# Memory keys and cross-attention queries of an encoder: high and low part of the moving operand side by side in 512 columns, the two halves added on the way out of PSUM

## The chip, the cores and the metric

The kernel runs on one core of a Trainium2 chip. The time is device microseconds of one execution; the number compared is the median of several runs. TensorE (PE) does the matmuls, VectorE (DVE) and ScalarE (ACT) the elementwise work, GpSimd (POOL) little here, and SyncE (SP) issues the loads. Sums of matmuls stand in PSUM, in banks of 128x512 numbers.

## The reference

Two layers of an encoder on 256 tokens of width 1024, with 256 tokens of memory. Cut to the part that matters here:

```python
for l in range(DEPTH):                       # DEPTH = 2
    h = hybrid_mixer(x, w_in[l], ...)
    x = layer_norm(alpha * x + h, ln_g[l, 0], ln_b[l, 0])
    h = memory_cross_attention(x, mem, xa_q[l], xa_kv[l], xa_o[l])
    x = layer_norm(alpha * x + h, ln_g[l, 1], ln_b[l, 1])
    h = conv_ffn(x, ffn_w_in[l], ...)
    x = layer_norm(alpha * x + h, ln_g[l, 2], ln_b[l, 2])

def memory_cross_attention(x, mem, xa_q, xa_kv, xa_o):
    q = (x @ xa_q).reshape(b, s, 4, 256) * 256 ** -0.5
    k, v = jnp.split(mem @ xa_kv, 2, axis=-1)
    p = softmax(q @ k^T)                     # per head
    return (p @ v).reshape(b, s, 1024) @ xa_o
```

The change touches `x @ xa_q` and the key half of `mem @ xa_kv`, 1024x1024 weights each, in both layers.

## The kernel before, in words

**Products.** Every f32 operand is split into a high part (a cast, L276, on ScalarE) and a low part (what is left, a subtraction, L277, on VectorE), and a product is three matmuls: high x high, high x low, low x high (`mm3`, L271 to L273). All weights pass once, in units of 128x1024 numbers (512 KB): SyncE's queue loads a unit into `raw`, ScalarE casts `hi`, VectorE subtracts `lo`. Seven units are prefetched, and eight `hi`/`lo` buffers exist.

**Two ways to use a unit.** Where the result is wanted with features on the partitions, `proj_f8` takes the unit's eight 128x128 blocks as stationary operands and the 256 tokens as the moving one: 24 matmuls of 256 columns into half a bank, so two units share one. The feed-forward uses `proj_twin` instead (L299, L301, L303). There the token activation is a `Twin`, which keeps high and low part of one block side by side, and one matmul of 512 columns multiplies the weight's high part with both: 8 matmuls of 512 columns, and 8 of 256 for the weight's low part times the high activation. A unit then fills a whole bank, with two halves that have to be added: `fold` copies one half out (L307, ScalarE) and adds the other to it (L308, VectorE). The accumulators `acc` are three banks; five more, `att`, hold transposes, attention and parts of the output projections.

**Stages.** Each layer: mixer, residual and LayerNorm, cross-attention, residual and LayerNorm, feed-forward, residual and LayerNorm. The LayerNorm (`ln`) of the two token tiles x_133 and x_134 takes sums (L409), a subtraction (L414), a reciprocal (L426) and a scaling (L419) on VectorE, with a square root on ScalarE (L410); TensorE then transposes the tile in pieces (L455), and each piece is split into high and low (L276, L277). Until then TensorE has no tokens for the next stage. The keys depend only on the memory, so their units fill such places: they stand in `fills`, and `main` allows some of them to be used at each LayerNorm. `split_keys` splits the finished keys (two tiles of 128x1024), ahead of the queries. The queries (`feat` under the name "xq") run right behind the LayerNorm, and after every two query units a head of the cross-attention is spawned (`cross_head`): scores, softmax (L871 to L879), transposes of the probabilities (L887), values.

**What sets the order.** `interleave` sets the steps one after another by rough costs. The framework then orders the instructions of each engine by a simulated schedule of its own; only SyncE's order is as written. LayerNorm operations are marked with `urgent`, and weight splits are kept `behind` them.

Of the kernel before, what the change touches and what calls it, by code (L numbers as in the profile page):

```python
# [111 lines left out]


def interleave(main, fills, banks):

    steps, done, active, pending = [], {}, [], []
    clock, free, nfill, allowed = 0.0, banks, 0, 0
    cur = next(main, None)

    def emit(s):  # L120
# [10 lines left out]
    while cur is not None or active:  # L131
# [23 lines left out]
        if isinstance(cur, Spawn):  # L155
            active.append([cur.name, clock + cur.delay, cur.gen, next(cur.gen)])
            cur = next(main, None)
            continue
# [66 lines left out]
class Encoder:  # L225
# [89 lines left out]
            self.mm3(o, xa.hi(kt + k, a, b), xa.lo(kt + k, a, b), hi[:, k], lo[:, k],  # L315
                     first and k == 0, last and k == 1)

    def feat(self, n, l, units, xn, evac):

        st = {}  # L320
        for i in range(units):
            def fn(u, i=i):
                if i % 2 == 0:
                    st["o"] = self.acc()
                o = st["o"]
                self.proj_f8(u, self.T[xn], o[:, 256 * (i % 2):256 * (i % 2) + 256])
                if i % 2:
                    evac(i // 2, o.rearrange("p (k t) -> p k t", k=2))
            yield Step(fn, U, units=[(n, l, i)])
# [135 lines left out]
    def fills(self):  # L465
        n = 0
        for l in range(DEPTH):
            def keys(l=l):
                for i in range(8):
                    def kfn(u, i=i):  # L470
                        if i == 0:
                            self.T["kT", l] = [self.big4() for _ in range(2)]
                        if i % 2 == 0:
                            self.T["ko"] = self.acc()
                        o = self.T["ko"]
                        self.proj_f8(u, self.T["mem"], o[:, 256 * (i % 2):256 * (i % 2) + 256])
                        if i % 2:
                            self.nc.scalar.copy(self.T["kT", l][i // 4][:, (i - 1) % 4:(i - 1) % 4 + 2],
                                                o.rearrange("p (k t) -> p k t", k=2))
                    yield ("k", l, i), Step(kfn, U, units=[("k", l, i)])  # L480

            def values(h, l=l):
                def evac(i, o):
                    if i == 0 and h == 0:
                        self.T["vM", l] = [[self.big(F32R) for _ in range(2)] for _ in range(2)]
                    vh, vl = self.T["vM", l]
                    sl = slice(512 * h, 512 * h + 512)
                    self.split_from(o, vh[i][:, sl], vl[i][:, sl])
                for s in self.tok("v", l, h, "mem", evac):
                    yield ("v", l, h), s  # L490

            parts = (values(0), keys(), values(1)) if l == 0 else (keys(), values(0), values(1))
            for p in parts:
                for k, s in p:
                    yield s
                    n += 1
                    self.nfill[k] = n
# [445 lines left out]
    def main(self):  # L943
        T = self.T
        allow = self.nfill
        yield Step(self.start)
        yield Allow(allow["k", 0, 3])
        for i in range(NT):
            yield Spawn(f"e{i}", self.ln(i, "xt00", 0, 15 + 5 * i))
        xn, lw = "xt00", ["e0", "e1"]  # L950
        for l in range(DEPTH):
            def lnc(j, l=l):
                return Step(lambda: self.ln_consts(self.aps["ln_g"][l, j], self.aps["ln_b"][l, j]))


            yield from self.tok_copy("va", l, xn, tiles=lw)
            if l == 0:
                yield Step(self.constants)
            rd = 6
            yield from self.feat_copy("qa", l, xn)  # L960
            yield Spawn(f"q{l}", self.rope("qa"), rd)
            yield from self.feat_copy("ka", l, xn)
            yield Spawn(f"k{l}", self.rope("ka"), rd)
            shs = [{"n": 0}, {"n": 0}, {"m": 0}]
            for i in range(NT):
                for g in range(2):
                    yield Spawn(f"dg{l}{i}{g}", self.diff_group(l, i, g, shs), 12)
            yield from self.tok_copy("vb", l, xn, split=True)
            yield from self.conv_branch(l, xn)
            yield from self.feat("qb", l, 4, xn, self.stack_evac("qb"))  # L970
            yield from self.feat("kb", l, 4, xn, self.stack_evac("kb"))
            yield Step(lambda l=l: self.bias_tiles(l, 0))
            for t in range(4):
                yield Spawn(f"na{l}{t}", self.near_pair(l, t), 1.0)
            yield from self.branch(l, 2, ("yc", l), xn, first=True)
            yield Wait(f"da{l}")
            yield from self.branch(l, 0, ("ya", l), xn)
            yield Wait(*(f"na{l}{t}" for t in range(4)))
            yield from self.branch(l, 1, ("yb", l), xn, last=True)
            yield lnc(0)  # L980
            yield Allow(max(allow["v", l, 0], allow["k", l, 7]))
            yield Step(self.load_mem)
            xn = f"xt{l}1"
            yield from self.residual(self.tok_out("mo", l, ("mg", l)), f"m{l}", xn)

            yield Wait(f"m{l}0", f"m{l}1")
            yield Allow(allow["v", l, 1])

            def evac(q, o):
                if q == 0:  # L990
                    T["qx"] = Act([self.big4(F32R)], [self.big4(F32R)])
                elif q == 2:
                    T["qx"].his.append(self.big4(F32R))
                    T["qx"].los.append(self.big4(F32R))
                f = 2 * (q % 2)
                self.split_from(o, T["qx"].his[-1][:, f:f + 2], T["qx"].los[-1][:, f:f + 2])
            yield Step(lambda l=l: self.split_keys(l))
            for n, s in enumerate(self.feat("xq", l, 8, xn, evac)):
                yield s
                if n % 2:  # L1000
                    yield Spawn(f"x{l}{n // 2}", self.cross_head(l, n // 2), 1.0)
            yield Wait(*(f"x{l}{h}" for h in range(4)))
            yield lnc(1)
            yield Allow(allow["k", 1, 3])
            xn = f"xt{l}2"
            yield from self.residual(self.tok_out("xo", l, ("oT", l)), f"a{l}", xn)

            um = l == DEPTH - 1
            if um:
                yield Step(self.keep_warm, acq=1, rel=1)  # L1010
                yield from self.up_first(l, xn, [f"a{l}0", f"a{l}1"])
            yield Wait(f"a{l}0", f"a{l}1")
            yield from self.ffn_in(l, xn, 4 if um else 0)
            yield Allow(allow["k", 1, 7])
            last = l == DEPTH - 1
            xn = None if last else f"xt{l + 1}0"
            lw = [f"f{l}0", f"f{l}1"]
            yield from self.residual(self.ffn_out(l), f"f{l}", xn)
        yield Wait(*lw)
# [239 lines left out]
```

## Time and profile before

| | |
|---|---|
| median of 3 runs | 1127.05 us (1126.41 to 1127.45) |
| profiled execution | 1126.91 us |
| its span in the trace | 1125.1 us |
| mean granted clock of TensorE | 0.994 |
| busy: TensorE / VectorE / ScalarE / GpSimd | 1094.9 / 833.2 / 643.4 / 12.4 us |
| loads | 208.45 MB, 185 GB/s over the span |

In the rows that follow, a row of a timeline has the start, the duration, engine, line, operation, output<-input, the size, how many such instructions stand together, and in brackets the idle time of the engine ahead of it and what ended it. A row of the groups has the busy time, the mean in ns, and the idle time in front with its releaser. Consecutive matmuls overlap, so their price is the distance between their starts, not the duration.

### The profile page before, as it was taken

The page shows a single profiled execution, that of the slowest core. Times are in us where ns is not written, and L with a number is a line of the kernel's source. Part 1 is how long each engine was busy: PE and PEld are TensorE (multiplying, and loading weights), DVE is VectorE, ACT ScalarE, POOL GpSimd, SP SyncE. Part 2 cuts the span into 40 slices and gives each one's busy share as a digit, 9 for nine tenths or more (in the row PEclk, how much of TensorE's full clock was granted, in tenths as well). Part 3 has the DMA queues.
Part 4 walks back from the last instruction along what each step waited for, and adds up shares of the span by engine and source line. Part 5 has one row for each costly group of instructions (what it writes and reads, how often), then busy time and mean ns, then how long its engine had stood idle before and what let it go on. Part 6 is the DMA issues. An engine that isn't in the chain of part 4 may idle for free.

```text
span 1125.1 us, 17377 instructions
## 1 busy us (share of the span) xinstructions
PE 1094.9 (97%) x6668; PEld 978.2 (87%) x6668; DVE 833.2 (74%) x1300; ACT 643.4 (57%) x1060; POOL 12.4 (1%) x18
## 2 busy tenths in 40 slices
PE   7999999999999999999999999999999978999997
PEld 6899998888998988888899999888889877888886
DVE  6887888566965988885586878965787576888744
ACT  5656667445553576665445666744536436666640
POOL 0000000000000000000000000000000000000001
PEclk9999999999999999999999999999999989999999
DMA  8775437567463576666747544556746344565651
GB/s 299 269 250 164 134 139 234 174 196 248 153 205 98 177 229 189 187 189 190 265 148 240 167 147 154 196 181 200 246 158 200 131 150 150 170 192 187 195 174 38
DMA packets 60466, 208.45 MB, mean 185 GB/s; under 512 B 7008, under 2 KB 8288, under 8 KB 60384
## 3 DMA queue, kind: packets, MB, share of 16 engines
q1 hardware_dynamic: 59952, 206.83, 57.0%
q8 instruction: 52, 0.85, 0.3%
q10 hardware_dynamic: 432, 0.52, 0.1%
q14 instruction: 30, 0.25, 0.1%
HBM read 204.18 MB, written 1.05 MB: 182 GB/s over the span
## 4 chain that ended last, share of the span: by engine, by line
PE 92%; DVE 3%; ACT 2%; DMA 1%; issue 1%; SPq 0%; DVEq 0%; ACTq 0%
PE acc L272 18%; PE acc L271 18%; PE acc L273 18%; PE acc L303 12%; PE acc L301 7%; PE att L272 4%; PE att L273 4%; PE att L271 4%; PE acc L299 2%; DVE lo L277 1%; DMA raw<-in_w_dram 1%; PE att L455 1%; PE att L653 1%; PE att L568 1%; DVE x L414 1%
## 5 line engine op out<-in xcount | busy, mean ns | idle before, releaser
L277 DVE TENSOR_TENSOR lo<-raw,hi 128x1024 fp32r<-128x1024 f32 x355 | 432.2, 1223 | 186.9 <-ACT hi L276 180.7
L276 ACT CAST hi<-raw 128x1024 fp32r<-128x1024 f32 x355 | 371.4, 1051 | 223.5 <-PE acc L273 75.3
L271 PE MATMUL acc<-hi,big 128*128 128x512 f32 x584 | 230.3, 396 | 6.6 <-ACT hi L276 6.6
L272 PE MATMUL acc<-lo,big 128*128 128x512 f32 x584 | 230.1, 394 | 0.3 <-DVE lo L277 0.3
L273 PE MATMUL acc<-hi,big 128*128 128x512 f32 x584 | 227.5, 392 | 0.0
L271 PE MATMUL acc<-big,hi 128*128 128x256 f32 x704 | 200.3, 285 | 3.2 <-ACT big L335 2.4
L273 PE MATMUL acc<-big,lo 128*128 128x256 f32 x704 | 200.5, 285 | 0.8 <-DVE lo L277 0.8
L272 PE MATMUL acc<-big,hi 128*128 128x256 f32 x704 | 200.0, 284 | 0.2 <-DVE big L277 0.2
L303 PE MATMUL acc<-big,hi 128*128 128x512 f32 x588 | 149.2, 393 | 0.0
L271 PEld LDWEIGHTS acc<-big,hi 128*128 128x128 f32 x704 | 134.6, 191 | 4.4 <-ACT big L335 2.8
L273 PEld LDWEIGHTS acc<-big,lo 128*128 128x128 f32 x704 | 134.8, 191 | 1.2 <-DVE lo L277 1.1
L272 PEld LDWEIGHTS acc<-big,hi 128*128 128x128 f32 x704 | 134.8, 191 | 0.8 <-DVE big L277 0.4
L271 PEld LDWEIGHTS acc<-hi,big 128*128 128x128 f32 x584 | 110.4, 189 | 27.0 <-ACT hi L276 7.0
L273 PEld LDWEIGHTS acc<-hi,big 128*128 128x128 f32 x584 | 110.5, 189 | 22.8
L272 PEld LDWEIGHTS acc<-lo,big 128*128 128x128 f32 x584 | 110.7, 190 | 21.2 <-DVE lo L277 1.2
L303 PEld LDWEIGHTS acc<-big,hi 128*128 128x128 f32 x588 | 105.1, 189 | 18.3
L301 PEld LDWEIGHTS acc<-big,lo 128*128 128x128 f32 x672 | 91.9, 190 | 6.7 <-ACT big L276 0.2
L301 PE MATMUL acc<-big,lo 128*128 128x256 f32 x672 | 94.1, 282 | 0.0
L272 PE MATMUL att<-lo,big 128*128 128x256 f32 (+1 forms) x228 | 72.6, 319 | 0.0
L271 PE MATMUL att<-hi,big 128*128 128x256 f32 (+1 forms) x228 | 72.4, 317 | 0.0
L273 PE MATMUL att<-hi,big 128*128 128x256 f32 (+1 forms) x228 | 72.3, 318 | 0.0
L307 ACT COPY t<-acc 128x256 f32<-128x256 f32 x84 | 31.2, 372 | 65.1 <-PE acc L303 65.1
(154 smaller groups left out, 1228.8 us busy)
## 6 DMA issues: line engine op xcount, KB each, us to landing
raw<-in_w_dram SPq DMA_DIRECT2D x355, 512.0 KB, 4.3
t<-in_bias_dram SPq DMA_DIRECT2D x16, 256.0 KB, 5.3
big<-in_ln_g_dram SPq DMA_DIRECT2D x6, 512.0 KB, 5.7
big<-in_ln_b_dram SPq DMA_DIRECT2D x6, 512.0 KB, 6.5
raw<-in_memT_dram SPq DMA_DIRECT2D x6, 512.0 KB, 4.8
big<-big SPq DMA_DIRECT2D x16, 128.0 KB, 2.3
x<-in_x_dram SPq DMA_DIRECT2D x4, 256.0 KB, 7.6
t<-in_memT_dram SPq DMA_DIRECT2D x3, 256.0 KB, 7.3
```

What stands on the lines that cost most here:

```text
L271: mm(o, lh, rh, start=first, stop=False)
L272: mm(o, lh, rl, start=False, stop=False)
L273: mm(o, ll, rh, start=False, stop=last)
L276: return (self.nc.scalar.copy(ah, src), self.nc.vector.tensor_tensor(out=al, in0=src, in1=rd(ah), op=ALU.subtract))
L277: self.nc.vector.tensor_tensor(out=al, in0=src, in1=rd(ah), op=ALU.subtract))
L299: mm(o, hi[:, 0], xa.both(0), start=True, stop=False)
L301: mm(o[:, S:], lo[:, k], xa.hi(k), start=False, stop=False)
L303: mm(o, hi[:, k], xa.both(k), start=False, stop=k == KT - 1)
L307: self.nc.scalar.copy(dst, o[:, S:])
L414: return nc.vector.scalar_tensor_tensor(out=x[:, sl], in0=x[:, sl], scalar=mv[:, 0:1], in1=self.lng[:, sl], op0=ALU.subtract, op1=ALU.mult)
L455: nc.tensor.transpose(pt[:, k], self.x[i][:, (n * h + k) * P:(n * h + k + 1) * P], self.ident)
L568: self.nc.tensor.matmul(o, q[m][:, h, t], k[2 + m][:, h], start=False, stop=True)
```

## The change

The keys and the cross-attention queries of both layers, 8 + 8 units in each, are computed with `proj_twin` and `fold` instead of `proj_f8`. A key unit is folded straight into its place in `kT`, where before a copy took two units out at once. For the queries a new flag `twin` of `feat` folds two units into one temporary tile of 128x512, from which the high and the low part are split; before they were split from PSUM. Each unit takes an accumulator bank of its own, where two units shared one. The mixer's units, the values and the output projections stay as they are. The lines of the changed kernel are shifted: the LayerNorm's subtraction, scaling and reciprocal are L421, L426 and L433 there, its transposes L462, and the lines of `cross_head` are higher by one.

```diff
@@ -315,11 +315,18 @@
             self.mm3(o, xa.hi(kt + k, a, b), xa.lo(kt + k, a, b), hi[:, k], lo[:, k],
                      first and k == 0, last and k == 1)
 
-    def feat(self, n, l, units, xn, evac):
+    def feat(self, n, l, units, xn, evac, twin=False):
 
         st = {}
         for i in range(units):
             def fn(u, i=i):
+                if twin:
+                    if i % 2 == 0:
+                        st["t"] = self.t512().rearrange("p (k t) -> p k t", k=2)
+                    self.fold(st["t"][:, i % 2], self.proj_twin(u, self.T[xn]))
+                    if i % 2:
+                        evac(i // 2, st["t"])
+                    return
                 if i % 2 == 0:
                     st["o"] = self.acc()
                 o = st["o"]
@@ -470,13 +477,7 @@
                     def kfn(u, i=i):
                         if i == 0:
                             self.T["kT", l] = [self.big4() for _ in range(2)]
-                        if i % 2 == 0:
-                            self.T["ko"] = self.acc()
-                        o = self.T["ko"]
-                        self.proj_f8(u, self.T["mem"], o[:, 256 * (i % 2):256 * (i % 2) + 256])
-                        if i % 2:
-                            self.nc.scalar.copy(self.T["kT", l][i // 4][:, (i - 1) % 4:(i - 1) % 4 + 2],
-                                                o.rearrange("p (k t) -> p k t", k=2))
+                        self.fold(self.T["kT", l][i // 4][:, i % 4], self.proj_twin(u, self.T["mem"]))
                     yield ("k", l, i), Step(kfn, U, units=[("k", l, i)])
 
             def values(h, l=l):
@@ -995,7 +996,7 @@
                 f = 2 * (q % 2)
                 self.split_from(o, T["qx"].his[-1][:, f:f + 2], T["qx"].los[-1][:, f:f + 2])
             yield Step(lambda l=l: self.split_keys(l))
-            for n, s in enumerate(self.feat("xq", l, 8, xn, evac)):
+            for n, s in enumerate(self.feat("xq", l, 8, xn, evac, twin=True)):
                 yield s
                 if n % 2:
                     yield Spawn(f"x{l}{n // 2}", self.cross_head(l, n // 2), 1.0)
```

The order of loads on SyncE and the work of GpSimd are the same. On the other engines the order moves at many places; three of them follow, all on VectorE. Names are those of tiles: `x_134` the second token tile, `big_` tiles of 128x1024 (activations, keys, LayerNorm constants), `lo_`/`hi_`/`raw_` of weights, `acc_` and `att_` PSUM banks, `t_` temporary tiles, `s_` small ones.

VectorE ahead of the queries of layer 0, before; big_2793 holds a constant of the LayerNorm, big_3056 to big_3059 the tokens' next `Twin`, att_3153 and the following the transposes of x_134:

```order
L414 SCALAR_TENSOR_TENSOR x_134<-x_134,s_3069,big_2792 128x256 x4
L277 TENSOR_TENSOR big_3057<-att_3060,big_3057 128x2x128
L426 RECIPROCAL s_3070<-s_3070 128x1
L419 SCALAR_TENSOR_TENSOR x_134<-x_134,s_3070,big_2793 128x256 x4
L277 TENSOR_TENSOR lo_3085<-raw_3082,hi_3084 128x1024
L277 TENSOR_TENSOR big_3058<-att_3113,big_3058 128x2x128
L277 TENSOR_TENSOR big_3056<-att_3153,big_3056 128x2x128
L277 TENSOR_TENSOR big_3057<-att_3189,big_3057 128x2x128
L277 TENSOR_TENSOR big_3058<-att_3194,big_3058 128x2x128
```

The same place in the changed kernel; big_289 is the second half of the keys, big_288 the first, big_3026 to big_3029 the `Twin`, and att_3111 the first transposes of x_134:

```order
L277 TENSOR_TENSOR big_3028<-att_3077,big_3028 128x2x128
L433 RECIPROCAL s_3040<-s_3040 128x1
L308 TENSOR_TENSOR big_289<-acc_3092,big_289 128x256
L426 SCALAR_TENSOR_TENSOR x_134<-x_134,s_3040,big_2769 128x256 x4
L277 TENSOR_TENSOR lo_3055<-raw_3052,hi_3054 128x1024
L277 TENSOR_TENSOR big_3029<-att_3077,big_3029 128x2x128
L277 TENSOR_TENSOR lo_3089<-raw_3086,hi_3088 128x1024
L277 TENSOR_TENSOR big_3158<-big_288,big_3156 128x1024
L308 TENSOR_TENSOR big_289<-acc_3122,big_289 128x256
L277 TENSOR_TENSOR big_3026<-att_3111,big_3026 128x2x128
```

A fold (L308) now stands ahead of the LayerNorm's scaling, and two weight splits, the split of the first half of the keys and another fold stand between the scaling and the first split of x_134's transposes.

VectorE ahead of the feed-forward of layer 0, before; big_3739 is a LayerNorm constant, big_3941 the first tile of the `Twin`, att_3945 transposes of x_133, att_4040 of x_134:

```order
L414 SCALAR_TENSOR_TENSOR x_134<-x_134,s_3954,big_3738 128x256 x4
L426 RECIPROCAL s_3955<-s_3955 128x1
L419 SCALAR_TENSOR_TENSOR x_134<-x_134,s_3955,big_3739 128x256 x4
L277 TENSOR_TENSOR lo_3970<-raw_3967,hi_3969 128x1024
L277 TENSOR_TENSOR big_3941<-att_3945,big_3941 128x2x128
L277 TENSOR_TENSOR big_3941<-att_4040,big_3941 128x2x128
```

The same place in the changed kernel; att_3857 and att_3906 are transposes of x_133, att_3940 the first of x_134, big_3885 the first half of layer 1's keys:

```order
L433 RECIPROCAL s_3867<-s_3867 128x1
L277 TENSOR_TENSOR big_3853<-att_3857,big_3853 128x2x128
L426 SCALAR_TENSOR_TENSOR x_134<-x_134,s_3867,big_3651 128x256 x4
L277 TENSOR_TENSOR lo_3882<-raw_3879,hi_3881 128x1024
L277 TENSOR_TENSOR big_3854<-att_3857,big_3854 128x2x128
L308 TENSOR_TENSOR big_3885<-acc_3887,big_3885 128x256
L277 TENSOR_TENSOR big_3855<-att_3906,big_3855 128x2x128
L308 TENSOR_TENSOR big_3885<-acc_3921,big_3885 128x256
L308 TENSOR_TENSOR big_3885<-acc_3951,big_3885 128x256
L277 TENSOR_TENSOR big_3853<-att_3940,big_3853 128x2x128
```

A split of transposed tokens (big_3853) has moved ahead of the scaling of x_134, and three folds stand behind it. On TensorE the fourth key unit now stands behind the transposes of x_134, right ahead of the feed-forward, where before it stood in front of them.

VectorE at the first head of the cross-attention of layer 1, before; att_8917 holds its scores, t_8934 its probabilities, s_ its maxima and sums:

```order
L277 TENSOR_TENSOR big_8883<-acc_8892,big_8882 128x512
L871 TENSOR_REDUCE s_8930<-att_8917 128x2
L872 TENSOR_SCALAR s_8930<-s_8930 128x2
L277 TENSOR_TENSOR lo_9038<-raw_9035,hi_9037 128x1024
L877 RECIPROCAL s_8931<-s_8931 128x2
L879 TENSOR_SCALAR t_8934<-t_8934,s_8931 128x256 x2
L277 TENSOR_TENSOR lo_9091<-raw_9088,hi_9090 128x1024
L277 TENSOR_TENSOR big_9066<-acc_8978,big_9065 128x512
```

The same place in the changed kernel, where att_8766 holds the scores and t_8783 the probabilities:

```order
L277 TENSOR_TENSOR big_8737<-t_8746,big_8736 128x512
L872 TENSOR_REDUCE s_8779<-att_8766 128x2
L277 TENSOR_TENSOR lo_8925<-raw_8922,hi_8924 128x1024
L873 TENSOR_SCALAR s_8779<-s_8779 128x2
L878 RECIPROCAL s_8780<-s_8780 128x2
L880 TENSOR_SCALAR t_8783<-t_8783,s_8780 128x256 x2
L308 TENSOR_TENSOR t_8822<-acc_8823,t_8822 128x256
L308 TENSOR_TENSOR t_8822<-acc_8880,t_8822 128x256
```

The weight split stands between the maximum (L872) and its scaling (L873), where before it stood behind the two; two folds follow the probabilities. On TensorE one query unit stands between these scores and the transposes of the probabilities, where more than two stood before.

## The prediction

> **What bounds the kernel now.** I read the head of the page first, then the chain of waits, the waits of TensorE, the costliest groups, and last the timelines of the places where the changed units stand.
>
> ```profile
> span 1125.1 us, 17377 instructions
> PE 1094.9 (97%) x6668; PEld 978.2 (87%) x6668; DVE 833.2 (74%) x1300; ACT 643.4 (57%) x1060; POOL 12.4 (1%) x18
> PE 92%; DVE 3%; ACT 2%; DMA 1%; issue 1%; SPq 0%; DVEq 0%; ACTq 0%
> PE att L455 <- DVE x L419: 6.6, 2, 6.2
> ```
>
> TensorE is busy for 97% of the span and carries 92% of the chain that ended last. Its waits in the list of waits come to some 22 us in all, most of them at the start and at one LayerNorm (the last row: two waits for LayerNorm pieces, 6.6 us, 6.2 of them at 917 to 923 us). So a matmul that goes saves its spacing, and a wait that appears on TensorE costs its length. VectorE has a quarter of its time free, but not at the places below, where it sets when TensorE may go on.
>
> The profiled execution took 1126.91 us, 1.8 us around its span of 1125.1, and 0.14 us under the median 1127.05. I sum against 1126.9. About 0.2% (2.3 us) is what can be told from no change: 1124.8 to 1129.3.
>
> **What the matmuls save.** An old unit issues 24 matmuls of 256 columns; the twin form issues 8 of 512 and 8 of 256. Both are in the trace, the second in the feed-forward. Starts, then durations:
>
> ```profile
> 299.67 0.28 PE L271 MATMUL acc<-big,hi 128*128 128x256 f32 x1
> 299.79 0.28 PE L272 MATMUL acc<-big,hi 128*128 128x256 f32 x1
> 299.91 0.28 PE L273 MATMUL acc<-big,lo 128*128 128x256 f32 x1
> ...
> 387.88 0.39 PE L299 MATMUL acc<-big,hi 128*128 128x512 f32 x1
> 388.11 1.11 PE L301 MATMUL acc<-big,lo 128*128 128x256 f32 x8
> 389.06 1.78 PE L303 MATMUL acc<-big,hi 128*128 128x512 f32 x7
> 390.67 0.39 PE L299 MATMUL acc<-big,hi 128*128 128x512 f32 x1
> ```
>
> Old: starts 0.12 us apart, 24 x 0.12 = 2.88 us. Twin: from 387.88 to the next unit at 390.67, 2.79 us. The columns that stream are the same 6144; what goes is eight issues. The difference, 0.085 us with the third decimal of the spacings, times 32 units (two layers, eight of keys and eight of queries) is 2.7 us. That is all the change can gain. The Trainium skill ("TensorE: Matmul & The Clock Gate", Back-to-back issue gap) gives N/2.4 + 2.5 ns for one matmul after another, that is 20 ns for eight issues fewer and, by that estimate, 0.6 us for 32 units. The trace's 0.12 us against 0.23 decides here.
>
> **What the fold adds.** A unit's two halves are added by a ScalarE copy and a VectorE add, for each unit, where one copy of 0.59 us served two units of keys and none was needed for the queries:
>
> ```profile
> L307 ACT COPY t<-acc 128x256 f32<-128x256 f32 x84 | 31.2, 372 | 65.1 <-PE acc L303 65.1
> L308 DVE TENSOR_TENSOR t<-acc,t 128x256 f32<-128x256 f32 x84 | 35.3, 421 | 10.8 <-ACT t L307 10.8
> L478 ACT COPY big<-acc 128x512 f32<-128x512 f32 x8 | 4.7, 588 | 6.7 <-PE acc L273 6.7
> ```
>
> VectorE gets 32 adds of 0.42 us (0.34 when they follow each other). In the steady stages this costs nothing: per unit VectorE has 1.14 (the weight's low part), 0.34 and at most another 0.34 of splitting, against 2.79 us on TensorE. The weight splits and the order of loads on the DMA queue stay. Feed-forward, mixer and output projections keep their matmuls. What costs is the order on VectorE at LayerNorms, where keys are the filling and the adds now stand in the chain. Four places, each by the order of after walked through with before's durations.
>
> **The first LayerNorm (28 to 32 us).**
>
> ```profile
> 28.11 1.80 PE L455 MATMUL att<-ident,x 128*128 128x128 f32 x12 [0.39 <-DVE x L419]
> 31.39 0.39 PE L273 MATMUL acc<-big,lo 128*128 128x256 f32 x1 [0.80 <-DVE lo L277]
> 27.22 2.99 DVE L419 SCALAR_TENSOR_TENSOR x<-x,s,big 128x512 f32<-128x512 f32 x6
> 30.12 3.49 DVE L277 TENSOR_TENSOR lo<-raw,hi 128x1024 fp32r<-128x1024 f32 x3
> ```
>
> TensorE goes on at 31.39 when VectorE's low part is there. An add now stands between two scalings (L419) ahead of it: the wait ends 0.34 us later, with the copy some 0.4. What the four key units before it save (0.34) is lost in that wait. New waiting: 0.76.
>
> **Layer 0, the LayerNorm before the queries (294 to 305 us).**
>
> ```profile
> 300.03 1.03 PE L455 MATMUL att<-ident,x 128*128 128x128 f32 x8
> 301.14 0.62 PE L271 MATMUL acc<-big,hi 128*128 128x256 f32 x3
> 296.94 1.67 DVE L419 SCALAR_TENSOR_TENSOR x<-x,s,big 128x256 f32<-128x256 f32 x4
> 298.53 1.22 DVE L277 TENSOR_TENSOR lo<-raw,hi 128x1024 fp32r<-128x1024 f32 x1
> 299.67 0.42 DVE L277 TENSOR_TENSOR big<-att,big 128x256 fp32r<-128x256 f32 x1
> 301.12 1.75 DVE L277 TENSOR_TENSOR big<-att,big 128x256 fp32r<-128x256 f32 x5 [1.03 <-ACT big L276]
> 305.44 1.22 DVE L277 TENSOR_TENSOR big<-big,big 128x1024 fp32r<-128x1024 f32 x1
> ```
>
> Before, the last scalings end at 298.5, then come one weight split and one split of transposed tokens, and VectorE is free (1.03 us) when the last transposes end at 301.0; the queries start at 301.14. In the changed order the first add stands ahead of the scalings. It waits for the last key unit but one, which ends at 297.0, and for its copy (0.37), so with the hand-overs it ends at about 298.3 and the scalings (1.67) at 300.0. TensorE is through its last key unit at 299.8 and through the eight transposes at 300.7. The query needs the first split of x_134's transposes, and ahead of that stand, on VectorE: weight split 1.14, token split 0.34, weight split 1.14, the split of the keys 1.14 (it had stood behind the start of the queries, at 305.4), an add 0.34. Then the split itself, 0.42. 300.0 + 4.5 = 304.5. TensorE waits 3.8 us where the transposes and the next unit had been 0.67 apart: 3.1 us more.
>
> **Layer 0, the LayerNorm before the feed-forward (371 to 388 us).**
>
> ```profile
> 383.23 0.82 PE L455 MATMUL att<-ident,x 128*128 128x128 f32 x6
> 384.72 0.48 PE L299 MATMUL acc<-big,hi 128*128 128x512 f32 x1
> 379.41 1.67 DVE L419 SCALAR_TENSOR_TENSOR x<-x,s,big 128x256 f32<-128x256 f32 x4
> 382.14 0.42 DVE L277 TENSOR_TENSOR big<-att,big 128x256 fp32r<-128x256 f32 x1
> ```
>
> Before, four key units run up to 383.2, x_134's transposes follow and the feed-forward starts at 384.72. Counted back over four units of 2.88 and x_133's eight transposes (0.87), the first unit starts at 370.84. From there three key units of the twin form (8.37 us) end at 379.2 and x_133's transposes at 380.1. x_134's scalings stand behind a token split that needs those transposes, so they start at 380.6, and the last transposes end at 382.55: 1.6 us without work. The fourth unit then needs an accumulator, and there are three. The add that frees the first one stands behind the scalings, a weight split and a token split: 382.3 + 1.14 + 0.34 + 0.34 = 384.1, another 1.6. The unit takes to 386.95, so the first feed-forward unit ends at 389.74 for 387.88. That is 1.86 later with four units' gain (0.34) inside: 2.2 us of new waiting.
>
> **Layer 1, the first head of the cross-attention (860 to 869 us).**
>
> ```profile
> 862.50 0.69 DVE L871 TENSOR_REDUCE s<-att 128x2 f32<-128x512 f32 x1 [0.45 <-PE att L273]
> 864.54 1.23 DVE L277 TENSOR_TENSOR lo<-raw,hi 128x1024 fp32r<-128x1024 f32 x1 [1.14 <-ACT hi L276]
> 866.87 0.17 DVE L877 RECIPROCAL s<-s 128x2 f32<-128x2 f32 x1 [1.11 <-ACT t L875]
> 867.07 0.62 DVE L879 TENSOR_SCALAR t<-t,s 128x256 f32<-128x256 f32 x2
> 864.52 1.28 ACT L875 ACT_TABLE_LOAD   x1
> 865.82 0.48 ACT L875 ACTIVATE t<-att,s 128x256 f32<-128x256 f32 x1
> ```
>
> Before, more than two units of query matmuls stand between the scores (over by 862.50, when the maximum starts) and the transposes of the probabilities, and cover the softmax: no wait of TensorE is listed there. After, one stands there (2.79), and a weight split (1.14) has got between the maximum and its scaling. From the end of the scores: maximum 0.65, split 1.14, scaling 0.17, table load 1.28, two exponentials 0.95, reciprocal 0.17, first half of the scaling 0.35, and some 0.4 of handing over: 5.1. Less 2.79 is 2.3 us of waiting.
>
> **Sum.** 1126.9 - 2.7 + 0.76 + 3.1 + 2.2 + 2.3 = 1132.6.
>
> **The clock.** Two stretches in which TensorE had been idle are in the trace. Columns: window, length, busy PE, PEld, DVE, ACT, POOL, then the granted clock.
>
> ```profile
> 11.31 0.98 PE L271 MATMUL acc<-hi,big 128*128 128x512 f32 x2 [2.07 <-ACT hi L276]
> 12.00:15.00 3.00, 2.72 (x7) 1.97 (x7) 2.92 (x5) 2.54 (x3) 0.00 (x0) 0.50 1.06 414
> 923.38 1.09 PE L455 MATMUL att<-ident,x 128*128 128x128 f32 x4 [6.20 <-DVE x L419]
> 923.00:926.00 3.00, 2.62 (x13) 2.65 (x14) 3.00 (x9) 0.46 (x2) 0.00 (x0) 0.50 0.52 176
> ```
>
> After both the clock was 0.50 for about 3 us, which takes 1.5 us from TensorE where it is the limit. An idle time of 3.8 us lies between 2.07 and 6.20. I count 1.5 us, with bounds of 0 (VectorE paces the queries' start anyway) and 1.7: 1134.1. The Trainium skill ("TensorE: Matmul & The Clock Gate", Part 1: The HAM clock gate) says that the clock is halved after an idle window of about 3.4 us. By that rule 3.8 us is just enough, and the shorter waits of the other places are not; the trace's 0.50 after 6.20 us agrees.
>
> **The rivals.**
>
> *No fall of the clock.* The waits come as worked out, but the 3.8 us at 301 us do not bring the clock down, or VectorE hides it. 1132.6. The idle time follows 200 us of full work, the 2.07 us one only the start; that speaks for it. Chance 0.20, against 0.42 for the forecast.
>
> *Waits half as long.* VectorE's rows ahead of the queries run partly before TensorE is through its transposes, since a quarter of its time is free. Half of 8.4 us of waiting less 2.7 is +1.5: 1128.4, no difference. Chance 0.12.
>
> *VectorE keeps pace: faster.* The adds and the moved splits all fit into the gaps that VectorE has (1.03 us ahead of 301.12, 1.14 and 1.11 around 865), and only the saving is left: 1126.9 - 2.7 = 1124.2. It decides at the first query of layer 0: if its split of x_134 ends by 301.1, this is what happens. Against it: 1.03 us is free there, and 3.0 us of rows (two adds of 0.34, splits of 1.14 and 1.14) are added ahead of it; from 296.94 to 300.1 VectorE runs without a gap. For it: at each of the other key units the fold is well covered. Chance 0.15.
>
> *More falls of the clock.* The waits before the feed-forward (1.6 + 1.6 with transposes between) also halve the clock: 1134.1 + 1.5 to 3 is 1136 to 1137. Chance 0.07.
>
> *The 512-column form saves nothing here.* A unit stays at 2.88 because the moved rows of two tiles come later, or VectorE holds its second operand. Then the 2.7 is missing: 1136.8. The feed-forward's 2.79 speaks against it. Chance 0.04.
>
> **How the numbers follow.** The likeliest is the forecast, 1134.1. Faster by over 0.2%: 0.15. Within: 0.12. Slower: 0.42 + 0.20 + 0.07 + 0.04 = 0.73. The range leaves out the fast rival and a little at the top: 1126.5 to 1137.0. The slower cases alone would span 1131 to 1137.
>
> **What would show it.** Right: PE waits of L299 for a split by VectorE (L277) of about 3.8 us near 301 us, for the LayerNorm's scaling (now L426) and for the add (L308) of 1.6 us each near 381 and 384, of the transposes (L888) for the scaled probabilities (L880) of 2.3 us near 866; a dip of the clock behind the first; 116 matmuls at L299 and adds at L308, 2.79 us apart. Wrong: the first query of layer 0 starting within 1.5 us of x_134's last transpose; no L308 among the releasers; or the waits there and the clock still 1.00 right behind. If the four waits come to less than 3 us in all, the forecast's mechanism is wrong, not its size.

## The result, and the profile after

The changed kernel takes 1135.52 us (median of 6, 1133.71 to 1136.62), the kernel before 1127.14 (6 runs): ratio 1.0072, 95% interval 1.0063 to 1.0082. It is slower by 8.4 us; 1134.1 was forecast, in a range of 1126.5 to 1137.0. The profiled execution took 1134.46 us, 7.55 more than that of before. Two executions further down, of 1357.61 and 1365.51 us at a mean granted clock of 0.751, are left out of the medians.

The head of the page and the chain of the changed kernel:

```profile
span 1132.6 us, 16929 instructions
PE 1095.5 (97%) x6412; PEld 965.7 (85%) x6412; DVE 842.6 (74%) x1332; ACT 649.9 (57%) x1084; POOL 12.4 (1%) x18
PE 87%; DVE 6%; DMA 3%; ACT 2%; issue 2%; SPq 1%; DVEq 0%; ACTq 0%
```

256 matmuls are gone (8 for each of 32 units), as the change says, and TensorE is no less busy (1095.5 us for 1094.9); its busy time counts the slower clock too, which makes up part of it. VectorE's share of the chain has grown from 3% to 6%, TensorE's has fallen from 92% to 87%. TensorE's waits show where, three of them new (total, times, longest):

```profile
PE acc L299 <- DVE big L277: 3.5, 1, 3.5
PE att L888 <- DVE t L880: 2.2, 1, 2.2
PE att L462 <- DVE big L277: 1.5, 1, 1.5
PE acc L301 <- DVE lo L277: 1.1, 1, 1.1
```

**Ahead of the queries of layer 0.** TensorE, then VectorE, in the timeline of after:

```profile
298.52 1.03 PE L462 MATMUL att<-ident,x 128*128 128x128 f32 x8
303.06 0.80 PE L299 MATMUL acc<-big,hi 128*128 128x512 f32 x1 [3.51 <-DVE big L277]
...
296.62 0.41 DVE L308 TENSOR_TENSOR big<-acc,big 128x256 f32<-128x256 f32 x1
296.94 1.67 DVE L426 SCALAR_TENSOR_TENSOR x<-x,s,big 128x256 f32<-128x256 f32 x4
298.52 1.22 DVE L277 TENSOR_TENSOR lo<-raw,hi 128x1024 fp32r<-128x1024 f32 x1
299.66 0.42 DVE L277 TENSOR_TENSOR big<-att,big 128x256 fp32r<-128x256 f32 x1
299.99 1.22 DVE L277 TENSOR_TENSOR lo<-raw,hi 128x1024 fp32r<-128x1024 f32 x1
301.12 1.22 DVE L277 TENSOR_TENSOR big<-big,big 128x1024 fp32r<-128x1024 f32 x1
302.26 0.42 DVE L308 TENSOR_TENSOR big<-acc,big 128x256 f32<-128x256 f32 x1
302.59 0.42 DVE L277 TENSOR_TENSOR big<-att,big 128x256 fp32r<-128x256 f32 x1
```

The add stands ahead of the scaling, and from the scaling's end at 298.5 VectorE works without a gap through the five rows that were counted, to the split at 302.59 that the query waits for. The transposes end at 299.5, the query starts at 303.06: 4.5 us from the transposes' start to the query, where before it was 1.1 (300.03 to 301.14).

**Ahead of the feed-forward of layer 0**, TensorE:

```profile
381.69 1.03 PE L462 MATMUL att<-ident,x 128*128 128x128 f32 x8
383.60 1.23 PE L462 MATMUL att<-ident,x 128*128 128x128 f32 x6 [0.88 <-DVE x L426]
386.35 0.41 PE L462 MATMUL att<-ident,x 128*128 128x128 f32 x2 [1.52 <-DVE big L277]
386.59 0.49 PE L299 MATMUL acc<-big,hi 128*128 128x512 f32 x1
389.48 0.39 PE L299 MATMUL acc<-big,hi 128*128 128x512 f32 x1
```

0.88 and 1.52 us, then the fourth key unit (386.59) and the first feed-forward unit (389.48).

**At the first head of layer 1**, VectorE and TensorE:

```profile
870.07 0.69 DVE L872 TENSOR_REDUCE s<-att 128x2 f32<-128x512 f32 x1 [1.27 <-PE att L273]
870.67 1.22 DVE L277 TENSOR_TENSOR lo<-raw,hi 128x1024 fp32r<-128x1024 f32 x1
871.81 0.16 DVE L873 TENSOR_SCALAR s<-s 128x2 f32<-128x2 f32 x1
...
875.01 0.33 PE L888 MATMUL att<-ident,t 128*128 128x128 f32 x1 [2.17 <-DVE t L880]
```

The weight split lies between the maximum and its scaling, and TensorE stands still for 2.17 us.

**The clock**, in windows of the changed kernel (columns as in the prediction; the first window is one that stood at 0.50 in before):

```profile
12.00:15.00 3.00, 3.00 (x14) 2.45 (x14) 2.36 (x4) 2.48 (x3) 0.00 (x0) 1.00 1.05 411
302.00:305.00 3.00, 1.94 (x8) 1.84 (x9) 3.00 (x7) 1.24 (x2) 0.00 (x0) 0.62 0.78 264
305.00:308.00 3.00, 3.00 (x18) 2.75 (x18) 2.40 (x3) 0.00 (x0) 0.00 (x0) 0.81 0.76 195
875.00:878.00 3.00, 2.99 (x17) 2.91 (x18) 2.99 (x6) 1.66 (x3) 0.00 (x0) 0.69 0.00 0
```

The clock fell behind the waits at 301 and at 873 us, each time to half for 3.4 us (302.7 to 306.1 and 876.2 to 879.6). It did not fall at the start of this execution, where that of before had lost such a stretch (11.6 to 15.0).

Where the difference arises, by the same instruction in the two traces:

| | before | after | difference |
|---|---|---|---|
| mixer of layer 0 (L568, now L569) | 152.65 | 151.12 | -1.5 |
| last head of layer 0 (transposes L887, now L888) | 351.30 | 353.75 | +2.5 |
| mixer of layer 1 (L568, now L569) | 628.21 | 632.43 | +4.2 |
| last head of layer 1 | 897.49 | 904.85 | +7.4 |
| end of the span | 1125.1 | 1132.6 | +7.5 |

Behind the last head nothing is added. The -1.5 comes from the start: the first key unit begins at 21.56 us before and at 19.61 after. 0.8 us of that was there before the clock differed, because a weight was ready earlier (the matmul that waits for it starts at 11.31 and at 10.49); the other 1.1 go with the half clock of before. The first LayerNorm takes 0.4 us of this back.

### The profile page after: what moved, and what is told of

Its sections match the earlier page's. It is cut to its first block, busy times and chain, and to the rows that moved or that the text cites. A ratio compares the mean times of both kernels' runs of the same rounds, so it can differ in the third digit from the quotient of the medians.

```text
span 1132.6 us, 16929 instructions
## 1 busy us (share of the span) xinstructions
PE 1095.5 (97%) x6412; PEld 965.7 (85%) x6412; DVE 842.6 (74%) x1332; ACT 649.9 (57%) x1084; POOL 12.4 (1%) x18
## 4 chain that ended last, share of the span: by engine, by line
PE 87%; DVE 6%; DMA 3%; ACT 2%; issue 2%; SPq 1%; DVEq 0%; ACTq 0%
PE acc L303 16%; PE acc L271 15%; PE acc L272 15%; PE acc L273 15%; PE acc L301 9%; PE att L272 4%; PE att L273 3%; PE att L271 3%; PE acc L299 2%; DVE lo L277 2%; DMA raw<-in_w_dram 2%; DVE x L421 1%; ACT hi L276 1%; DVE x L426 1%; DMA big<-in_emb_ln_b_dram 1%
## 5 line engine op out<-in xcount | busy, mean ns | idle before, releaser
L303 PE MATMUL acc<-big,hi 128*128 128x512 f32 x812 | 207.4, 393 | 0.0
L303 PEld LDWEIGHTS acc<-big,hi 128*128 128x128 f32 x812 | 145.1, 189 | 25.0
L301 PEld LDWEIGHTS acc<-big,lo 128*128 128x128 f32 x928 | 129.1, 193 | 11.7 <-DVE lo L277 1.8
L301 PE MATMUL acc<-big,lo 128*128 128x256 f32 x928 | 132.6, 285 | 2.1 <-DVE lo L277 1.1
L271 PE MATMUL acc<-big,hi 128*128 128x256 f32 x448 | 127.5, 285 | 2.4 <-ACT big L342 2.4
L273 PE MATMUL acc<-big,lo 128*128 128x256 f32 x448 | 127.9, 285 | 0.0
L272 PE MATMUL acc<-big,hi 128*128 128x256 f32 x448 | 127.4, 285 | 0.0
L271 PEld LDWEIGHTS acc<-big,hi 128*128 128x128 f32 x448 | 85.7, 191 | 3.1 <-ACT big L342 2.8
L272 PEld LDWEIGHTS acc<-big,hi 128*128 128x128 f32 x448 | 85.7, 191 | 0.2
L273 PEld LDWEIGHTS acc<-big,lo 128*128 128x128 f32 x448 | 85.7, 191 | 0.2
L307 ACT COPY t<-acc 128x256 f32<-128x256 f32 x100 | 37.0, 373 | 80.2 <-PE acc L303 80.0
```

The lines of the kernel that those rows point to most:

```text
L271: mm(o, lh, rh, start=first, stop=False)
L272: mm(o, lh, rl, start=False, stop=False)
L273: mm(o, ll, rh, start=False, stop=last)
L301: mm(o[:, S:], lo[:, k], xa.hi(k), start=False, stop=False)
L303: mm(o, hi[:, k], xa.both(k), start=False, stop=k == KT - 1)
L307: self.nc.scalar.copy(dst, o[:, S:])
```

## The experiments

The theory: the matmuls save 2.7 us, and the changed order on VectorE at three places, with the clock behind it, costs more. Rivals: the fold costs something at every unit; one bank per unit is what makes the waits, whoever empties it; the 512-column form saves nothing. All times are medians beside runs of the kernel before on the same chip.

**e1_keys: the keys alone.** The queries stay as before (`twin=True` left out).

> Only the keys take the twin form and the fold; the queries stay as before. If the time goes at the LayerNorms and at the first head of layer 1: TensorE's waits near 301 us (3.5 us, with a fall of the clock behind it) and near 383 to 386 us (2.4 us in all) stay, the 2.2 us in front of the first head's transposes in layer 1 and the fall of the clock behind it go; 1135.5 - 3.9 for that head + 1.4 for the queries' lost saving = 1133.0. If the folds cost something at every unit (the rival: 8.4 us spread evenly over 32 units): half of it, 1131.3, and no wait of that length at one place.

1133.81 us, ratio 1.0068 (1.0054 to 1.0081). Its waits:

```profile
PE acc L271 <- DVE big L308: 2.7, 1, 2.7
PE att L462 <- DVE big L277: 1.5, 1, 1.5
```

The two LayerNorm places stay and the one at the head is gone, so the keys carry 6.9 of the 8.4 us, not half. The first row says something new: a high x high matmul of the first queries, now of the old form, waits for the fold (it starts at 304.10, the fold ends at 304.05), and it needs nothing from VectorE but a free bank. The split that the next matmul needs ends only 0.3 us later (304.38), so the bank is not the only thing that holds TensorE there.

**e2_queries: the queries alone**, with the keys as before.

> Only the queries take the twin form and the fold; the keys stay as before. If the time goes at the named places: no wait above 1 us near 301 or 383 us, and one of about 1 us at the first head of layer 1, since its order puts 4.2 us of query matmuls there against 5.1 us of softmax; 1127.1 - 1.4 + 1 = 1126.7, up to 1128.3 if the clock falls there. If the folds cost something at every unit: 1131.3.

1129.07 us, ratio 1.0016 (1.0007 to 1.0026): 2.1 us more than before. At 301 and 383 us no wait is longer than 0.5. None stands at the first head of layer 1, but one that was not expected does in layer 0:

```profile
325.45 0.47 PE L299 MATMUL acc<-big,hi 128*128 128x512 f32 x1 [1.53 <-DVE t L308]
```

A query unit waits for a bank, whose fold stands behind the softmax on VectorE. That eats the 1.4 us that 16 units save. With the 0.5 at 302 us the new waits less the saving come to some 0.7 us, just under the interval (0.8 to 2.9 us); in the profiled execution another 1.0 us stands at the start, ahead of any query (the same matmul at 91.45 and 90.42), so where the rest comes from is not shown. The even cost (1131.3) is out for both runs.

**e5_banks and c_before_banks: four accumulators and four banks of the other kind**, in the changed kernel and in the one before:

```diff
-    ACC, ATT = 3, 5
+    ACC, ATT = 4, 4
```

> The changed kernel with four accumulator banks and four of the other kind, for three and five. If one bank per unit, where two units shared one, is the root (the fourth unit of a run of keys has no bank until VectorE has added the first one's halves): the fourth key unit stands ahead of the transposes again, the wait near 383 to 386 us goes, two query units stand at the first head and its wait goes, the one near 301 us falls to 1.5 to 2 us without a fall of the clock: 1127.1 - 2.7 + 0.8 + 1.8 = 1127.0, give or take 1. If only VectorE's load at the LayerNorms matters, and not the banks: within 1 us of 1135.5.

> The kernel before with four accumulator banks and four of the other kind: the control for the run with four banks and the change. Its units share banks in pairs, so a fourth should bring nothing: 1127.1, up to 1128.5 where one bank fewer for transposes and attention is missed. If it is faster by 5 us or more, the four banks help by themselves, and the run with both tells nothing of the change.

1143.78 us (ratio 1.0141, 1.0122 to 1.0161) and 1142.27 (1.0133, 1.0117 to 1.0148). Both expectations failed: the fifth bank of the other kind is worth 15 us to the kernel before, in the attention of the mixer. Its waits, then those of the changed kernel:

```profile
PE att L567 <- ACT big L554: 5.6, 2, 2.8
PE att L741 <- DVE t L733: 4.7, 3, 2.7
```

```profile
PE att L568 <- ACT big L555: 5.6, 2, 2.8
PE att L742 <- DVE t L734: 5.3, 4, 2.9
PE att L462 <- DVE big L277: 3.1, 3, 1.9
PE acc L299 <- DVE big L308: 0.2, 1, 0.2
```

Against each other they tell what was asked: with four accumulators the change costs 1.5 us in place of 8.4, and even that is not clear of the noise (1137.99 to 1144.28 with the change, 1140.00 to 1143.03 without). No query waits for a split by VectorE, no transpose for the probabilities, and four key units stand in one piece ahead of x_134's transposes again. The transposes wait 2.4 us in two pieces ahead of the queries. Since the order differs at many places, this points to the banks and doesn't prove them.

**e3_no_add: no add.** ScalarE copies the first half out; the other half is left out of keys and queries.

```diff
-                        self.fold(self.T["kT", l][i // 4][:, i % 4], self.proj_twin(u, self.T["mem"]))
+                        self.nc.scalar.copy(self.T["kT", l][i // 4][:, i % 4],
+                                            self.proj_twin(u, self.T["mem"])[:, :S])
...
-                    self.fold(st["t"][:, i % 2], self.proj_twin(u, self.T[xn]))
+                    self.nc.scalar.copy(st["t"][:, i % 2], self.proj_twin(u, self.T[xn])[:, :S])
```

> The changed kernel without the fold's add: ScalarE copies only the first half out, and the second half is left out of keys and queries. One bank per unit stays, but no VectorE instruction stands between a unit and its bank. If what costs is that VectorE's queue holds the banks: the wait for an accumulator goes, so the second of the waits near 383 to 386 us (1.5 us) and the one at the first head of layer 1 (2.2 us) with its fall of the clock (1.7) go, while the wait near 301 us stays at 2.8 (two adds of 0.34 less in front, the weight splits and the split of the keys still ahead): 1135.5 - 0.7 - 1.5 - 2.2 - 1.7 = 1129.4. If the adds alone are what costs: all waits go, 1124.4. If one bank per unit costs whoever empties it: within 1 us of 1135.5.

1131.28 us, ratio 1.0033 (1.0021 to 1.0045): still 3.8 us above before, with no instruction added on VectorE. The split of the keys and two weight splits stand ahead of the first query as in the change, and it waits 3.0 us; a query unit in layer 1 now waits for ScalarE's copy out of a bank (0.9):

```profile
PE acc L299 <- DVE big L277: 3.0, 1, 3.0
PE acc L299 <- ACT t L326: 0.9, 1, 0.9
```

So without the adds about half of it goes (8.4 to 3.8 us), and the order is not their doing alone.

**e9_bank_only: one bank and one copy per unit, with the old matmuls and nothing to add.**

```diff
-                        self.fold(self.T["kT", l][i // 4][:, i % 4], self.proj_twin(u, self.T["mem"]))
+                        o = self.acc()[:, :S]
+                        self.proj_f8(u, self.T["mem"], o)
+                        self.nc.scalar.copy(self.T["kT", l][i // 4][:, i % 4], o)
```

and the same in `feat`.

> Keys and queries with the 24 matmuls of 256 columns of before, no halves to add, but one bank and one ScalarE copy per unit, as in the change. It differs from the run without the add only in the matmuls. If one bank per unit brings the waits, whatever matmuls fill it: a wait of 2.5 to 3 us near 301 us and 1 to 1.5 us near 383 us, and 2.7 us above the run without the add: 1134.0 (1132.5 to 1135). If the waits come from the add, or from the faster units: 1127.1 to 1128.5, without these waits.

1129.22 us, ratio 1.0024 (1.0014 to 1.0034). It computes the same products as before; each unit has its own bank and its own copy by ScalarE, and the queries are split from the copied tile, no longer from PSUM. It has the waits: for the split ahead of the queries, and for a bank ahead of the feed-forward (a row of its timeline, then one of its waits).

```profile
301.01 0.39 PE L272 MATMUL acc<-big,hi 128*128 128x256 f32 x1 [1.52 <-DVE big L277]
```

```profile
PE acc L299 <- ACT big L484: 1.3, 1, 1.3
```

One bank per unit, with the copy that it brings, is thus a cause by itself, of 2.5 us. The other half of the expectation failed: the run without the add should be 2.7 below this one by its matmuls and is 1.3 above (3.8 and 2.5 us over the kernel before beside each); at the same mean clock, 0.995, the two are equal (1129.2, one execution, and 1129.0, four). In the same VectorE order its query waits 3.0 us where this one waits 1.5. The split ends 4.0 us behind the transposes' start without the add (298.27 to 302.24) and 3.0 us here (297.97 to 300.95), and the LayerNorm's subtraction starts 4.2 and 5.2 us ahead of them: TensorE has 1.0 us less to do in between. That is more than the shorter units explain (three by 0.085); the scheduler has also laid the work otherwise. So the 2.7 us of the wide form don't show in the total. At this place 1.0 us of cover is gone, and how much of that is the order stays open.

**e10_pairs: the price of the wide matmul.** Six of a unit's eight 512-column matmuls are taken apart, all else as in the change:

```diff
...
+        for k in range(1, KT - 1):
+            mm(o[:, :S], hi[:, k], xa.hi(k), start=False, stop=False)
+            mm(o[:, S:], hi[:, k], xa.lo(k), start=False, stop=False)
+        mm(o, hi[:, KT - 1], xa.both(KT - 1), start=False, stop=True)
```

> The change with six of a unit's eight matmuls of 512 columns taken apart into two of 256: banks, folds and operands as in the change, 22 matmuls per unit in place of 16. If the saving of the 512-column form is what the spacings say (0.085 us for eight, so 0.064 for six): a unit takes 2.85 us in a run of key units, and 32 units 2.0 us more. The waits near 301 and 383 us stay as in the change, since VectorE's order is the same there; at the first head of layer 1 two units stand now, so the wait of 2.2 us goes: 1135.5 + 2.0 - 2.2 less up to 1.5 of the clock there = 1134.5 (1133.5 to 1135.5). If the wide form saves nothing, a unit takes 2.79 and the total is 1132 to 1133.3.

1133.80 us, ratio 1.0061 (1.0046 to 1.0077). The starts of two key units in a row, here and then in the change:

```profile
378.54 0.39 PE L310 MATMUL acc<-big,hi 128*128 128x512 f32 x1
381.39 0.40 PE L310 MATMUL acc<-big,hi 128*128 128x512 f32 x1
```

```profile
376.10 0.39 PE L299 MATMUL acc<-big,hi 128*128 128x512 f32 x1
378.89 0.39 PE L299 MATMUL acc<-big,hi 128*128 128x512 f32 x1
```

2.85 against 2.79: the wide form saves what the spacings said. Yet this kernel, with 2 us more of matmuls, is no slower than the change (6.6 us over before, for 8.4): two query units now cover the first head of layer 1, and the 2.2 us there are gone.

**e8_fourth: every fourth key unit in a bank of the other kind.** The call alone:

```diff
-    self.proj_twin(u, self.T["mem"])
+    self.proj_twin(u, self.T["mem"], self.att() if i % 4 == 3 else None)
```

> The changed kernel with every fourth key unit in a bank of the other kind (five of them); the counts of banks stay. If the missing fourth accumulator keeps the fourth key unit behind the transposes ahead of the feed-forward of layer 0: it stands between them again, and of the 2.4 us of waits near 383 to 386 us at most 0.5 stays. In its order four matmuls rows more stand at the first head of layer 1, and the wait of 2.2 us goes there with its fall of the clock (1.7): 1135.5 - 2 - 2.2 - 1.7 = 1129.6; the wait near 301 us stays at 3.2 or more. If the waits come from VectorE's load and not from banks: within 1 us of 1135.5.

1131.37 us, ratio 1.0040 (1.0027 to 1.0053): half of the loss comes back when four units use another bank. The fourth key unit of layer 1 stands between the transposes again:

```profile
383.55 0.83 PE L462 MATMUL att<-ident,x 128*128 128x128 f32 x4 [0.88 <-DVE x L426]
384.14 0.48 PE L299 MATMUL att<-big,hi 128*128 128x512 f32 x1
387.03 0.38 PE L462 MATMUL att<-ident,x 128*128 128x128 f32 x2
387.87 0.44 PE L462 MATMUL att<-ident,x 128*128 128x128 f32 x2 [0.45 <-DVE big L277]
```

The waits there are 1.3 us for 2.4, and the wait at the first head of layer 1 is gone. Ahead of the queries of layer 0 the 3.5 us have become 1.6 and 1.4, and one wait of 1.5 us for a bank at a query unit is new, most of the 1.8 us by which the expectation was missed.

**e7_mend: that, and the keys' split behind the second query unit.**

> The same with the keys' split set behind the second query unit in each layer. Ahead of the first query of layer 0 then stand two weight splits and a token split, but neither the keys' split (1.14) nor the second add (0.34): the wait near 301 us falls from 3.5 to about 2.0, the waits near 383 us and at the first head are covered. 1127.1 - 2.7 + 0.8 at the first LayerNorm + 1.4 = 1126.6, up to 1128.3 if the clock falls behind the 2.0 us. If the folds cost time wherever they stand, it is no better than 1131.

1131.52 us, ratio 1.0040 (1.0027 to 1.0052). Ahead of the first query of layer 0 the waits are 1.6 and 0.2 us, as expected, but nothing is won in all. Query units now wait for banks at two heads:

```profile
PE acc L299 <- DVE t L308: 4.5, 4, 1.5
```

Four such waits, of which the kernel before has two of 0.7. At the two new ones (326.8 and 875.4 us) a softmax on VectorE holds up a fold and so a bank. No version that was run beats the kernel before.

**e6_warm and e6b_warm15: TensorE kept busy at 301 us**, by 30 and then 15 matmuls on the identity.

```diff
             yield Step(lambda l=l: self.split_keys(l))
+            if l == 0:
+                yield Step(lambda: self.keep_warm(15), acq=1, rel=1)
```

> The changed kernel with 30 matmuls of 128 columns on the identity, whose result is not used, behind the last transposes ahead of layer 0's queries: TensorE works through the 3.5 us in which it waited near 301 us. If the idle time brings the clock down and that costs 1 to 1.7 us: the clock stays 1.00 from 302 to 306 us, the first three query units come 1 to 1.7 us earlier, and the total is 1134.2 (1133.8 to 1134.5) although TensorE does more. If the clock falls for another reason, or VectorE sets the pace there anyway: 1135.5, with the same start of the later units.

> The run with matmuls on the identity again, with 15 of them: in the first, 30 stood in the trace as 60 of 0.115 us and held TensorE for 6.9 us, 3.9 longer than the wait that they were to fill. 15 fill 3.5 us. If the idle time brings the clock down there and this costs 1 to 1.7 us: no half clock between 300 and 307 us in any execution, and a median of 1134.2 (1133.8 to 1134.8) for 1135.5. If VectorE sets the pace of the first query units anyway, the clock stays up and the median is 1135.5.

1139.36 us (ratio 1.0104, 1.0090 to 1.0117) with 30, 1135.71 (1.0078, 1.0065 to 1.0091) with 15. The first overfilled the gap by 3.9 us and is 3.8 us slower than the change. The second fits, and the clock stays up there; then it falls behind the next waits (its timeline, then its windows):

```profile
302.08 3.59 PE L1042 MATMUL att<-ident 128*128 128x128 f32 x30 [0.67 <-DVE big L277]
```

```profile
302.00:305.00 3.00, 2.92 (x26) 2.95 (x27) 3.00 (x5) 2.48 (x6) 0.00 (x0) 1.00 0.62 194
387.00:390.00 3.00, 2.64 (x13) 2.47 (x14) 3.00 (x10) 2.19 (x4) 0.00 (x0) 0.69 0.61 171
```

From the transposes' start to the fourth query unit it is 13.5 us (300.38 to 313.89) for 14.4 in the change (298.52 to 312.89): 0.9 us from the clock at this place, although the matmuls end 0.5 us late. In the total nothing is left. The idle time brings the clock down, and its price there is nearer to 1 than to 1.5; but with 15 matmuls the clock falls at 388 us, where it did not in the change, and not at 876, where it did, and the time is no lower.

## Why the prediction was right, point by point

**The matmuls** save 2.7 us: right, by 2.79 us per unit in the change and 2.85 with six matmuls taken apart. The trace decided rightly against 0.6 us.

**The first LayerNorm** (0.76 us): right. The wait for the weight's low part is 1.1 us for 0.8, and from the first key unit to the mixer at 88 us the changed kernel loses 0.4 us (21.56 to 88.27 before, 19.61 to 86.72 after): the 0.76 less the 0.34 of four units. Ahead of the first key unit this pair of executions differs by 1.95 us in favour of the change, before any changed unit has run; that is one reason why the profiled difference, 7.55, is smaller than that of the medians.

**Ahead of the queries** (3.8 us of waiting and a fall of the clock): 3.51 us and the fall, row for row. From layer 0's mixer to its last head the trace gives +4.0 (-1.5 to +2.5); the terms come to 3.1 + 1.5 - 0.085 x 12 units = 3.6.

**Ahead of the feed-forward** (1.86 us later): right in the sum, wrong in the waits. From the start of the first key unit (373.29; 370.84 before) to the start of the second feed-forward unit (392.27; 387.88 before) it is 1.9 us longer than before. The first wait is 0.88 us, not 1.6. The fourth unit did not wait for an accumulator, as the step had it. The last transposes waited 1.52 us for a token split, and when they were through the add had just freed the bank (386.53; the unit starts at 386.59).

**The first head of layer 1** (2.3 us): 2.17, right. What failed is the step on the clock, which put one fall behind 3.8 us only and gave "more falls", behind the waits ahead of the feed-forward, 0.07. The clock fell behind 2.17 us as well, so from the mixer to the last head of layer 1 the loss is 3.2 us, for 1.5 by the terms without it. That missing fall is most of what the forecast is short of in these traces: from the first key unit to the end they lose 9.5 us, for 7.2 in the sum. That the profiled difference, 7.55, stands so near to the forecast's 7.2 is luck of the start.

The length of an idle time was the wrong measure. In the 13 traces of this case every change of the clock lies on a fixed raster of 3.41 us that runs through the execution, and whether a stretch of the raster stands at half goes by the busy time of TensorE in the stretch before it. Here are the stretch with the 2.17 us and the one behind it, in the changed kernel:

```profile
872.73:876.15 3.42, 1.25 (x11) 1.15 (x11) 1.71 (x6) 3.35 (x9) 0.00 (x0) 1.00 0.55 153
876.15:879.56 3.41, 3.41 (x18) 3.31 (x17) 2.94 (x5) 1.29 (x3) 0.00 (x0) 0.50 0.39 91
```

TensorE was busy for 0.37 of the first, and the second stood at 0.50. Ahead of the fall at 302.7 us the share was 0.08, ahead of the one at the start of before, behind the 2.07 us that the prediction shows, 0.39. Over all 13 traces, with the clock at full speed, a share below 0.5 was followed by half clock each time, one above 0.56 never, and shares from 0.51 to 0.56 both ways. So a wait of 2.17 us is enough when it lies within one stretch, and where the stretches begin differs between executions. The two waits at 383 us are at the limit: the share is 0.55 in the change, without a fall, and 0.55 with the 15 matmuls, with one (0.69 at 387 us). The Trainium skill ("TensorE: Matmul & The Clock Gate", Part 1: The HAM clock gate) speaks of a free-running activity window of some 3.4 us. The raster agrees with that; but the window need not be idle throughout, as the prediction took it when it held 3.8 us to be just enough.

**The cause.** The prediction took the order on VectorE as given and named the three accumulators for one wait only. The runs go one step further back. One bank per unit, with the old matmuls and no add, has the same kind of waits (+2.5 us); giving one key unit in four another bank brings half of the loss back; leaving out the adds does so too. The adds, the shorter cover and the clock make up the rest of the 8.4. How they share it can't be settled, since each run changes the order again.

**The rivals.** "VectorE keeps pace" fell where it was to be decided: the first query's split ended at 303.0, 1.9 us behind the 301.1 that it needed, in a trace whose transposes came 1.5 us earlier. "No fall of the clock" and "the wide form saves nothing" fell too.

## What to carry to other kernels

A saving of issues on the busiest engine is real but small, and it shortens the cover of everything that the other engines do beside it: price the places where that engine goes on only after a chain on another. Before a result takes a whole bank in place of half of one, count the units that must be in flight at the narrowest place and what stands in the queue of the engine that frees them. Where a kernel's LayerNorms are filled with spare matmuls, walk the new order there with durations of the trace: here that gave the three places, and a total within 1.5 us. Judge what a wait does to the clock by how busy TensorE is over some 3.4 us, not by the length of the wait alone.

## What the runs showed of the hardware that was not expected

The granted clock differs between executions of the same kernel, and the time with it: of 51 executions of the kernel before that were run beside the experiments, 28 with a mean clock of 0.994 took 1127.25 us on average, 15 with 0.995 took 1125.61. One stretch of 3.4 us at half clock is 0.0015 of the span. The changed kernel's six have 0.991 to 0.994, and 1133.71 us at 0.994: against 1127.25 at the same clock that is 6.5 us more (one execution only), which leaves, as an estimate, some 2 of the 8.4 for the falls of the clock that its waits bring about.

A matmul on the f32 identity stands in the trace as two, of 0.115 us each (15 as 30 in 3.59 us).
